# The first two blocks of an input projection become a pair with one group of seven products, and the recurrence behind them starts three steps later

## The chip, the cores and the metric

The kernel runs on one core of one Trainium2 chip. The time is device microseconds of that core for one execution; a stated time is the median of several runs. The engines are PE (TensorE, matrix products into PSUM accumulators), DVE (VectorE), ACT (ScalarE), POOL (GpSimd) and SP (SyncE, which here only issues transfers). Each engine works through its own list of instructions in order and waits at an instruction until what it needs is there.

## The reference

One layer of an encoder on x of 256 rows and 2048 columns, in float32. In short:

```
x += 1/2 * SwiGLU(RMSNorm(x))                       # F = 5632 columns
h = RMSNorm(x);  [u | q | k | v] = h @ w_in         # w_in: 2048 x 4096, u, q, k, v of 1024 each
y_ssm = GLU(S5(u))                                  # a diagonal complex recurrence over the rows
y_sb  = StickBreakingAttention(norm(q), norm(k), v)
x += concat(RMSNorm(y_ssm), RMSNorm(y_sb)) @ w_out
x += 1/2 * SwiGLU(RMSNorm(x))
x += RMSNorm((p @ w_ple_proj) * sigmoid(RMSNorm(x) @ w_ple_gate))
```

The change touches `u = h @ w_in[:, :1024]` and when the recurrence S5(u) begins.

## The kernel before

**Products.** A float32 product is made from three products of a reduced type. Each operand is split into a high part (a rounded copy, a cast on ACT) and a low part (the difference, on DVE): `split`, lines 182 and 185. PE then adds up left-high times weight-high, left-low times weight-high (line 345) and left-high times weight-low (line 340). The left side is the activation, normed only by its gain; the row scale of the RMSNorm (`xn.rs(t)`) is applied when the accumulator is read. The 256 rows are two row tiles (t = 0, 1) of 128.

**Blocks, quarters, halves.** Weight columns are worked in blocks of 512. The 2048 rows of a weight are 16 k tiles, four to a quarter. SP loads a quarter (`raw`, 1 MB, five buffers, of which two hold x through this stage); it is split in halves of two k tiles (`weight_pair`, tiles `whi` and `wlo`, four of each). `gemm_block` runs a block: for each quarter it takes the activation's part, loads and splits the weight, and for each half issues 12 products of 512 columns (two row tiles, two k tiles, three products).

**Seven products.** Elsewhere in this kernel (the two FFNs and the final gate) two blocks are a pair (`Seven`). On one k quarter, with the two k halves, the two row tiles and the two blocks as a 2 x 2 by 2 x 2 product, `chunk` makes seven products in place of eight, in Winograd's form. It needs sums of weights: `t1 = b11 + b12`, `t2 = t1 + b22`, `t4 = t2 + b21` on DVE, and `b12 + b22` by a transfer that adds into SBUF, issued by POOL (line 597). It needs sums of the activation, made by `whole_rows` and `sum_forms` (line 486). Each of the seven has its own split, and is 6 products of 512 columns into one of eight accumulator banks: 1, 2, 4 and 5 are the four `acc` buffers, 6 with 7 and 3 with 8 the two double `aux` buffers. `column` runs quarters of one block of the pair in the plain way. What comes out is then put together: `opened` (bank 1, 6, 7), `gated` (2, 4, 5), and a last sum with banks 3 and 8. In the FFNs `weight_pair` takes three further pairs from a second pool (`ring`, `turns`); `single`, a form of `chunk`, runs with the four alone.

**Steps.** `step()` is called behind each half of a plain block, and four times in a `chunk`. `put_off(n, fn)` runs fn in the (n+1)-th step from then. So everything beside the main products is placed by counting steps: the RMSNorm's parts (`Normed`), the recurrence, the attention. From this program order a planner makes each engine's list, by what it reckons to be ready; instructions under `pin` keep their order.

**Around the change.** After the first FFN `s5_main` sets the recurrence up, then two blocks make u, then four blocks q0, k0, q1, k1, then two blocks v: 16, 32 and 16 steps. Quarter 3 of the normed x comes through PE transposes two steps after the FFN's last block (line 435), the other quarters through DVE transposes and transfers. `u_block` reads a block's two accumulators with the row scale (line 1121). `u_turn` (line 1127) transposes the result in blocks of 32, and `u_part` (line 1138) moves it by eight transfers on SP into `ua[n]`, where the recurrence reads it. The recurrence has four quarters q; each is a chain of stages counted from `a0 = 13 + 8 * q`: `states` (PE, line 1186), `forth` (1203), `scan` (1213), `back`, `outputs` (PE, 1241), `fetch`, `join`, `gelu`. It keeps three tiles `rt` in turn. Its constants come by transfers from scratch memory: `m1`, `rot`, `cp` on SP (line 1151), and `m3` from `scr_h` on POOL (line 1159). Behind the last `gelu`, `channels` sends the result through 32 transfers on SP (line 1287) into `zt`, four a step; `glu_in` reads it 11 steps behind the q and k blocks. `qk_turn` transposes q and k on PE into an `aux` buffer, five steps behind each of their blocks.

## Time and profile before

| what | value |
|---|---|
| median of 3 runs | 1814.45 us (1814.3 to 1815.05) |
| the profiled execution: its time, its span | 1816.04 us, 1814.3 us |
| PE busy | 1806.9 us, 8914 products |
| PE weight loads busy | 1497.1 us |
| DVE busy | 1573.8 us |
| ACT busy | 1065.2 us |
| POOL busy | 104.8 us |
| HBM read and written | 372.41 MB, 10.88 MB |
| first load of `w_in` issued | 681.4 us |
| first product of u | 705.95 us |
| first product of the recurrence | 746.37 us |
| first transfer of `zt` | 847.88 us |

The page of the profile shows one execution. A row of its groups, or of the order of time, names the line of the kernel, the engine, the operation, output and inputs by the program's names, and shapes. In the order of time the first two numbers are start and duration in us, and a bracket at the end gives how long the engine stood idle before it and what ended this. Records of products last 0.39 us and overlap, since PE works on several at once; the distance between starts is the pace. Waits are inferred from semaphores.

### The profile page before, as it was taken

What the parts mean: (1) busy time and instruction counts of PE and PEld (TensorE: products, weight loads), DVE (VectorE), ACT (ScalarE), POOL (GpSimd) and SP (SyncE); (2) the same over time, 40 slices, a digit from 0 to 9 for tenths busy, and PEclk for the clock granted to TensorE, in tenths of its full rate; (3) what the DMA queues carried; (4) which work ended last, traced back from release to release, by engine and by line L of the source; (5) the groups of instructions that cost most, each with busy time, mean ns of one, the idle gap of its engine ahead of it and who ended that gap; (6) DMA issues with size and microseconds to landing.
All of it is one profiled execution on the core that took longest, in us unless ns stands there. A gap on an engine that the chain in (4) does not pass through costs nothing.

```text
span 1814.3 us, 24211 instructions
## 1 busy us (share of the span) xinstructions
PE 1806.9 (100%) x8914; PEld 1497.1 (83%) x8914; DVE 1573.8 (87%) x1840; ACT 1065.2 (59%) x1240; POOL 104.8 (6%) x160
## 2 busy tenths in 40 slices
PE   9999999999999999999999999999999999999998
PEld 7888888888888888888898888888888888888887
DVE  7998889999998896697567899999999999889875
ACT  7445456555565665456695566555565556566664
POOL 0020100000000001010021000000000000000000
PEclk9999999999999999999999999999999999999999
DMA  9599867787776667674646787786767786666663
GB/s 369 201 307 318 255 225 232 240 269 221 257 269 218 197 234 253 189 254 156 219 146 217 232 295 228 265 271 221 234 232 238 242 271 239 227 209 223 200 244 128
DMA packets 107799, 428.41 MB, mean 236 GB/s; under 512 B 24512, under 2 KB 48352, under 8 KB 65280
## 3 DMA queue, kind: packets, MB, share of 16 engines
q1 hardware_dynamic: 96832, 391.15, 61.2%
q0 software_dynamic: 10560, 35.40, 9.0%
q8 instruction: 70, 1.15, 0.3%
q14 instruction: 49, 0.40, 0.1%
q10 hardware_dynamic: 288, 0.31, 0.1%
HBM read 372.41 MB, written 10.88 MB: 211 GB/s over the span
## 4 chain that ended last, share of the span: by engine, by line
PE 96%; DMA 2%; DVE 1%; SPq 1%; ACT 0%; issue 0%; ACTq 0%; DVEq 0%
PE acc L345 32%; PE acc L340 16%; PE aux L345 15%; PE aux L340 7%; PE acc L529 5%; PE acc L532 5%; PE acc L530 5%; PE aux L532 3%; PE aux L530 3%; PE aux L529 3%; DMA raw<-in_ffn_w_up 1%; SPq L233 0%; DMA sg<-in_turned 0%; PE aux L1241 0%; PE acc L1497 0%; PE acc L1492 0%
## 5 line engine op out<-in xcount | busy, mean ns | idle before, releaser
L185 DVE TENSOR_TENSOR wlo<-raw,whi 128x1024 fp32r<-128x1024 f32 x478 | 578.1, 1222 | 126.8 <-ACT whi L182 123.3
L182 ACT CAST whi<-raw 128x1024 fp32r<-128x1024 f32 x478 | 496.3, 1050 | 295.5 <-PE acc L345 182.7
L345 PE MATMUL acc<-whi,nhi 128*128 128x512 f32 x908 | 356.0, 393 | 0.4 <-ACT whi L297 0.3
L345 PE MATMUL acc<-whi,nlo 128*128 128x512 f32 x908 | 353.4, 390 | 0.0
L340 PE MATMUL acc<-wlo,nhi 128*128 128x512 f32 x908 | 252.9, 389 | 0.6 <-DVE wlo L185 0.5
L185 DVE TENSOR_TENSOR slo<-raw,shi 128x1024 fp32r<-128x1024 f32 x186 | 226.0, 1215 | 16.9 <-ACT shi L182 16.7
L182 ACT CAST shi<-raw 128x1024 fp32r<-128x1024 f32 x186 | 195.1, 1049 | 61.4 <-DMA raw<-in_ffn_w_down 22.3
L345 PEld LDWEIGHTS acc<-whi,nhi 128*128 128x128 f32 x908 | 170.5, 188 | 37.7 <-ACT whi L297 0.7
L340 PEld LDWEIGHTS acc<-wlo,nhi 128*128 128x128 f32 x908 | 170.5, 188 | 36.9 <-DVE wlo L185 1.4
L345 PEld LDWEIGHTS acc<-whi,nlo 128*128 128x128 f32 x908 | 170.8, 188 | 34.8
L182 ACT CAST whi<-sum 128x1024 fp32r<-128x1024 f32 x79 | 83.3, 1054 | 160.1 <-DVE sum L536 143.9
L182 ACT CAST shi<-sum 128x1024 fp32r<-128x1024 f32 x59 | 62.2, 1054 | 101.8 <-DVE sum L536 91.5
L536 DVE TENSOR_TENSOR sum<-sum,raw 128x1024 f32<-128x1024 f32 x92 | 112.1, 1219 | 0.9
L185 DVE TENSOR_TENSOR wlo<-sum,whi 128x1024 fp32r<-128x1024 f32 x79 | 96.2, 1220 | 5.3 <-ACT whi L182 4.5
L597 POOL DMA_DIRECT2D raw<-raw x44 | 38.2, 869 | 1032.6 <-DVE sum L536 714.6
L345 PE MATMUL aux<-whi,nhi 128*128 128x512 f32 x220 | 85.7, 390 | 0.0
L345 PE MATMUL aux<-whi,nlo 128*128 128x512 f32 x220 | 85.6, 389 | 0.0
L185 DVE TENSOR_TENSOR slo<-sum,shi 128x1024 fp32r<-128x1024 f32 x59 | 72.0, 1220 | 1.1 <-ACT shi L182 0.5
L340 PE MATMUL aux<-wlo,nhi 128*128 128x512 f32 x220 | 67.8, 389 | 0.0
L536 DVE TENSOR_TENSOR sum<-raw,raw 128x1024 f32<-128x1024 f32 x46 | 56.0, 1217 | 5.6 <-DMA raw<-in_ffn_w_down 4.6
L345 PE MATMUL acc<-whi,hhi 128*128 128x512 f32 x156 | 60.7, 389 | 0.0
L345 PE MATMUL acc<-whi,hlo 128*128 128x512 f32 x156 | 60.7, 389 | 0.0
(393 smaller groups left out, 3401.3 us busy)
## 6 DMA issues: line engine op xcount, KB each, us to landing
raw<-in_ffn_w_up SPq DMA_DIRECT2D x88, 1024.0 KB, 5.7
raw<-in_ffn_w_down SPq DMA_DIRECT2D x88, 1024.0 KB, 4.9
raw<-in_ffn_w_gate SPq DMA_DIRECT2D x86, 1024.0 KB, 7.2
raw<-in_w_in SPq DMA_DIRECT2D x32, 1024.0 KB, 5.3
raw<-raw POOLq DMA_DIRECT2D x46, 512.0 KB, 5.5
raw<-in_w_out SPq DMA_DIRECT2D x16, 1024.0 KB, 5.0
raw<-in_w_ple_gate SPq DMA_DIRECT2D x16, 1024.0 KB, 5.1
hT<-mid SPq DMA_DIRECT2D x160, 64.0 KB, 4.7
```

The lines of the kernel that those rows point to most:

```text
L182: copy = nc.scalar.copy(hi, src)
L185: rest = nc.vector.tensor_tensor(out=lo, in0=src, in1=hi.bitcast(F32), op=ALU.subtract)
L340: nc.tensor.matmul(ps[t], lhsT=lh, rhs=lo[:, j, cols], start=False, stop=stop and j == 1)
L345: nc.tensor.matmul(ps[t], lhsT=(ahi, alo)[i][:, 2 * h + j, t * P : (t + 1) * P], rhs=hi[:, j, cols], start=start and j == 0 and i == 0, st ...
L529: nc.tensor.matmul(ps, lhsT=lh[j], rhs=hi[:, j], start=begin and j == 0, stop=False)
L530: nc.tensor.matmul(ps, lhsT=ll[j], rhs=hi[:, j], start=False, stop=False)
L532: nc.tensor.matmul(ps, lhsT=lh[j], rhs=lo[:, j], start=False, stop=z in final and j == 1)
L536: nc.vector.tensor_tensor(out=t, in0=x, in1=y, op=ALU.add)
L597: nc.gpsimd.dma_start(b12, b22, accum_op=ALU.add)
```

## The change

The two blocks of u are no longer two calls of `gemm_block` and `u_block`, but one `u_pair` on both with kb = 3:

- side 0 in the plain way on quarters 0 and 1, then `made` (the sums of the activation's quarter 3), then quarter 2;
- the seven products on quarter 3 of both blocks, with the four weight pairs alone (`turns` is None, and `chunk` no longer sets the ring in that case);
- `opened` and `gated` put off to the next step: they read banks 1, 6, 7, 2, 4 and 5; side 0 of u is then scaled and goes to `u_turn`;
- side 1 on quarters 0, 1 and 2, a last sum with banks 3 and 8, scaling, `u_turn`.

The sums take the recurrence's three `rt` tiles (`Spare`). The steps stay 16: six, four and six. The loads of `m1`, `rot` and `cp` for the first quarter of the recurrence go from at once to 3, 6 and 9 steps put off, those of `m3` from 4 to 8, and `a0` from 13 to 16, and with it every stage of the recurrence, its later loads and `zt`.

```diff
-            if ring[0] is None:
+            if ring[0] is None and self.turns:
                 ring[:] = [self.turns, 0]
...
+    class Spare:
+        def __init__(self, pool):
+            self.pool = pool
+
+        def tile(self, shape, dtype, tag, name, bufs):
+            return get(self.pool, "rt", bufs=3).rearrange("p (j n) -> p j n", n=NB)
+
+    def u_pair(pool, xn, w, kb, forms):
+        rows = Spare(pool)
+        us = [com("sg"), com("h")]
+        even, odd = ([u[:, t * NB : (t + 1) * NB] for t in range(TT)] for u in us)
+
+        def made():
+            forms[kb] = sum_forms(rows, whole_rows(rows, xn(kb)), "h")
+
+        def opened(s):
+            nc.scalar.copy(even[0], s.bank(1))
+            nc.vector.tensor_tensor(out=odd[0], in0=s.bank(6), in1=even[0], op=ALU.add)
+            nc.vector.tensor_tensor(out=odd[1], in0=s.bank(7), in1=odd[0], op=ALU.add)
+
+        def scaled(side):
+            u = us[side]
+            for t in range(TT):
+                v = u[:, t * NB : (t + 1) * NB]
+                nc.scalar.activation(v, v, AF.Copy, scale=xn.rs(t))
+            put_off(1, u_turn, pool, side, u)
+
+        def gated(s):
+            for t, (ps, other) in enumerate(((s.bank(2), even[0]), (s.bank(4), odd[1]))):
+                nc.vector.tensor_tensor(out=even[t], in0=ps, in1=other, op=ALU.add)
+            scaled(0)
+            v = us[1].rearrange("p (t n) -> p t n", t=TT)
+            nc.vector.tensor_tensor(
+                out=v, in0=s.bank(5).unsqueeze(1).to_broadcast([P, TT, NB]), in1=v, op=ALU.subtract
+            )
+
+        others = tuple(k for k in range(ND) if k != kb)
+        s = Seven(xn, forms.get, ((w, 0), (w, NB)), rows, None)
+        s.column(0, others[:2])
+        made()
+        s.column(0, others[2:])
+        s.chunk(kb, (*shared, 2, 4))
+        put_off(0, opened, s)
+        put_off(0, gated, s)
+        s.column(1, others, True)
+        nc.vector.tensor_tensor(out=us[1], in0=s.banks[3.8], in1=us[1], op=ALU.add)
+        scaled(1)
...
-        load(0, ("m1", "rot", "cp"))
+        for i, name in enumerate(("m1", "rot", "cp")):
+            put_off(3 + 3 * i, load, 0, (name,))
         for z in range(SL):
-            put_off(4 + z, load_m3, z)
+            put_off(8 + z, load_m3, z)
...
-            a0 = 13 + 8 * q
+            a0 = 16 + 8 * q
...
-    for n in range(2):
-        u_block(pool, n, gemm_block(nm, w_in, n * NB, KD), nm)
+    forms = {}
+    u_pair(pool, nm, w_in, 3, forms)
```

## The prediction

> **What bounds the kernel now.** I read the page first (busy time, then the chain of work that ended last), then tables of busy time by stretch around the input projection, then the order of time of each engine there.

> ```profile
> span 1814.3 us, 24211 instructions
> ...
> PE 1806.9 (100%) x8914; PEld 1497.1 (83%) x8914; DVE 1573.8 (87%) x1840; ACT 1065.2 (59%) x1240; POOL 104.8 (6%) x160
> ...
> PE 96%; DMA 2%; DVE 1%; SPq 1%; ACT 0%; issue 0%; ACTq 0%; DVEq 0%
> ```

> TensorE (PE) is idle for 1814.3 - 1806.9 = 7.4 us in all, and 96% of the chain is its own. A busy PE need not be at its peak, so I look at the stage of the change: columns are PE, weight load, DVE, ACT, POOL (busy us, instructions), granted clock, DMA share, GB/s.

> ```profile
> 700.00:750.00 50.00, 50.00 (x282) 41.05 (x282) 27.15 (x38) 24.86 (x33) 6.08 (x12) 1.00 0.79 254
> ...
> 850.00:870.00 20.00, 20.00 (x90) 16.57 (x89) 8.48 (x14) 9.62 (x12) 0.00 (x0) 1.00 0.37 102
> ```

> PE has no idle time from 700 to 750 and its clock is full; DVE works 27.15 of these 50 us. So the time here is the number of PE products times their pace, plus whatever PE is made to wait. Two starts on the chain, one half quarter (12 products) apart, give the pace:

> ```profile
> 720.60 1.81 PE acc L345 x8
> 723.32 1.81 PE acc L345 x8
> ```

> (723.32 - 720.60) / 12 = 0.227 us for one product of 512 columns.

> **The change, part by part.** *Products of the last quarter.* Two blocks, four k tiles, two row tiles and three products each (hi hi, lo hi, hi lo) are 48; seven groups of two k tiles and three products are 42. Six products go: 6 x 0.227 = -1.36 us on the path. No transposes or other PE work come in. [...]

> *The sum forms of the left side.* `made` must wait for quarter 3 of the normed input. Before:

> ```profile
> 705.95 0.39 PE L345 MATMUL acc<-whi,nhi 128*128 128x512 f32 x1
> ...
> 707.96 1.05 ACT L182 CAST whi<-raw 128x1024 fp32r<-128x1024 f32 x1 [3.93 <-PE acc L345]
> ...
> 714.11 1.03 PE L435 MATMUL aux<-ident,x 128*128 128x128 f32 x8
> 714.90 0.48 PE L345 MATMUL acc<-whi,nhi 128*128 128x512 f32 x1
> ...
> 717.07 1.66 DVE L197 SCALAR_TENSOR_TENSOR nlo<-aux,gains,nhi 128x256 fp32r<-128x256 f32 x4 [0.25 <-ACT nhi L195]
> ```

> Quarter 3 is there at 717.07 + 1.66 = 718.7. The forms are one sum of 1024 elements, four small ones, a cast and a difference. The final gate stage builds the same ones, and only then begins the sums of its seven (L536):

> ```profile
> 1705.65 1.23 DVE L469 TENSOR_TENSOR whole<-nhi,nlo 128x1024 f32<-128x1024 f32 x1 [0.71 <-PE aux L340]
> ...
> 1708.04 0.42 DVE L486 TENSOR_TENSOR rows<-whole,rows 128x256 f32<-128x256 f32 x1
> ...
> 1710.21 1.18 DVE L185 TENSOR_TENSOR hlo<-rows,hhi 128x1024 fp32r<-128x1024 f32 x1
> ...
> 1713.17 1.21 DVE L536 TENSOR_TENSOR sum<-raw,raw 128x1024 f32<-128x1024 f32 x1
> ```

> From start to end 1710.21 + 1.18 - 1705.65 = 5.7 us there, with other DVE instructions before the difference. Without them: 1708.04 + 0.42 - 1705.65 = 2.8 for the five sums, 1.05 for the cast, 1.18: 5.0. So the forms are ready between 723.7 and 724.4. PE's need: the row at 714.90 starts half 3 of the first block; halves 4 and 5 follow at 717.62 and 720.34, so the seven begin at 714.90 + 3 x 2.72 = 723.06. Group 1 uses whole rows; group 5 starts at 723.06 + 1.36 = 724.4 and is the first to need the forms. The margin is between 0.7 us and nothing, so no wait if DVE takes the forms first.

> *Splits and sums of the seven.* Three more splits (cast 1.05 on ACT, difference on DVE) and three sums. DVE's pace in a row of such instructions:

> ```profile
> 237.86 4.62 DVE L185 TENSOR_TENSOR wlo<-raw,whi 128x1024 fp32r<-128x1024 f32 x4
> 242.40 0.68 DVE L1084 TENSOR_TENSOR m<-t,t 128x512 f32<-128x512 f32 x1
> ```

> (242.40 - 237.86) / 4 = 1.14 us each. The seven take DVE (7 + 3) x 1.14 = 11.4 us against 42 x 0.227 = 9.5 us on PE: DVE loses 1.9 us, which its lead must cover. The lead is four weight pairs (the change gives this group no extra ring): the cast at 707.96 waits for PE to release the pair of the half that began at 705.95, so splits run four places ahead. Four places before the seven are groups 1, 5, 6 and 4, 5.4 us of PE. Here the 4.0 us of forms on DVE fall into the same stretch. The accumulators are now read by DVE four times over 512 columns and twice over 1024; such reads cost:

> ```profile
> 1744.55 0.68 DVE L1638 TENSOR_TENSOR e<-acc,e 128x512 f32<-128x512 f32 x1
> ...
> 1746.22 1.23 DVE L1632 TENSOR_TENSOR e<-acc,e 128x1024 f32<-128x1024 f32 x1
> ```

> In all DVE gains 6 x 1.14 (splits, sums) + 4.0 (forms) + 4 x 0.68 + 2 x 1.23 = 16.0 us; 27.15 + 16.0 = 43 of 50, so it fits on average and is tight from 717 to 731.

> What the tightness costs is read from two places that run the seven. With four pairs only, in the first FFN (group starts):

> ```profile
> 230.06 0.39 PE L529 MATMUL acc<-whi,nhi 128*128 128x512 f32 x1
> ...
> 231.44 0.50 PE L529 MATMUL acc<-whi,hhi 128*128 128x512 f32 x1
> ...
> 232.95 0.39 PE L529 MATMUL acc<-whi,nhi 128*128 128x512 f32 x1
> ```

> 1.38 and 1.51 instead of 1.36: 0.17 us lost. At the gate stage's seven, the first column half behind them:

> ```profile
> 1728.58 0.41 PE L345 MATMUL acc<-whi,nhi 128*128 128x512 f32 x1
> ...
> 1730.33 0.39 PE L345 MATMUL acc<-whi,nhi 128*128 128x512 f32 x1
> ```

> (1730.33 - 1728.58) - 1.36 = 0.39 us lost. Bounds for this stage: nothing lost, to 6.1 us (second rival). I take +0.4, the gate stage's value, since it too has the forms just ahead. ACT's additions (four casts, one copy) lie in a stage where it is half idle.

> *Transfers.* Loads on SP stay the same in number. The pair needs quarter 3 of both blocks at once:

> ```profile
> 698.71 1.00 SPq L330 DMA_DIRECT2D raw<-in_w_in  x2
> 705.32 0.33 SPq L330 DMA_DIRECT2D raw<-in_w_in  x1
> 705.74 0.38 SPq L1151 DMA_DIRECT2D m<-scr_m  x1
> ...
> raw<-in_w_in SPq DMA_DIRECT2D x32, 1024.0 KB, 5.3
> raw<-raw POOLq DMA_DIRECT2D x46, 512.0 KB, 5.5
> ```

> These three issues now carry quarter 2 and both quarters 3, landed by 705.32 + 5.3 = 710.6, twelve us ahead; the recurrence's three loads leave this moment, which helps them. The one new transfer (a sum within SBUF, on POOL's queue) can start after the first sum and takes 5.5 us; its user is the last group, at 723.06 + 6 x 1.36 = 731.2. Even if that sum runs only at 722 the transfer is down by about 729. The `scr_h` loads stand behind it on POOL and are first read by `outputs`, much later. Zero.

> *The recurrence, three steps later.* The first inputs wait for the pair, whose first side is complete only when the seven end (723.06 + 9.5 = 732.6): then come four reads by DVE (2.7 us), two scalings by ACT, two transposes, eight issues and their landing:

> ```profile
> 728.85 1.26 ACT L1121 ACTIVATE sg<-acc,sm 128x512 f32<-128x512 f32 x2
> ...
> L1127 DVE STREAM_TRANSPOSE ub<-sg x4: 669/693/704, 730.1 to 756.8; 128x512 f32<-128x512 f32 x4
> ...
> DMA to landing us min/median/max: 2.2/2.4/4.9
> ...
> 731.45 5.00 SPq L1138 DMA_DIRECT2D ua<-ub  x8
> ...
> 746.37 0.32 PE L1186 MATMUL aux<-ua,m 64*64 64x64 f32 x2
> ```

> 732.6 + 2.7 + 1.3 + 1.4 + 5.0 + 2.4 = 745.4. `states(0)` moves from 746.37 by three steps less the saving, 8.2 - 1.4, to about 753. Covered by 7 us; if that cover were gone, each microsecond late is one on PE, which runs `states` in its own order. At the far end the 32 `zt` issues move too:

> ```profile
> 847.88 15.18 SPq L1287 DMA_DIRECT2D zt<-mid  x24
> 863.18 0.51 SPq L330 DMA_DIRECT2D raw<-in_w_in  x1
> ...
> 868.70 2.00 ACT L182 CAST whi<-raw 128x1024 fp32r<-128x1024 f32 x2 [6.74 <-DMA raw<-in_w_in]
> ...
> 871.76 0.48 PE L345 MATMUL acc<-whi,nhi 128*128 128x512 f32 x1
> ```

> A weight load of `v` stands behind 24 of them; its cast ends at 869.75 for a half that starts at 871.76, 2.0 us to spare. Later by three steps the block meets another load. Bounds: none, to all 32 ahead of one: 8 more at 15.18 / 24 = 0.63, less 2.0, is 3.0 us. I take zero: the issues go out four a step from step 52 on, and the next block's first load comes before step 57, behind 20 of them and not 24. The recurrence's DVE work ends some 7 us later, in or near 850 to 870, where DVE is free for 11.5 of 20 us. The loads of `m1`, `rot` and `cp` go onto SP at steps 4, 7 and 10 in place of at once: three issues of 0.4 us, whose users are `states` and later.

> **Sum.** -1.36 + 0.4 = -0.96 us: the profiled span 1814.3 becomes 1813.3, and its execution, 1816.04 with what lies around it, 1815.1. That execution is 1.6 us over the runs' median of 1814.45; on the median the sum gives 1813.5.

> **Rivals.** *The saving is eaten.* Small waits at the forms and in the seven together cost 1 to 3 us: 1814.1 to 1816.1. For it: DVE is short by 1.9 us over the seven, with the forms on top. Against: the two places above lost 0.17 and 0.39. *The forms stand behind the seven's own work (slower).* DVE runs what its planned order says. If the three sums and the splits of groups 1, 5 and 6 (6 x 1.14 = 6.8 us) precede the forms, group 5 starts 6.8 - 0.7 = 6.1 us late: 1814.45 - 1.36 + 6.1 = 1819.2. It turns against the change from 1.4 us of wait. Against: at the gate stage the forms came first (L486 and `hlo` before L536). [...] *The `zt` block starves the `v` products*: 1813.5 + 3.0 = 1816.5; against it, the order reckoned above. *The pair relieves the turning of q and k*: `states` and `outputs` no longer hold both wide accumulators when `qk_turn` wants one. PE shows no idle there to recover: 1813.1 at best.

> **How the numbers follow.** Forecast 0.62 and relief 0.04 (1812.8 to 1814.1), saving eaten 0.18, forms late 0.09, `zt` 0.04, something faster than any row explains 0.03. A measurement of this kernel tells about 0.2% (3.6 us) from no change: forecast, relief, eaten saving and most of `zt` lie within it, forms late above it. Hence faster 0.03, same 0.87, slower 0.10. The range goes from 1812.6, which is 1813.1 less half a microsecond of spread between runs, to 1816.4, which holds the eaten saving.

> **What would show it.** PE 8908 instructions; DVE about 1858; POOL 161. Seven group starts 1.36 apart near 723 to 732, with the forms' `hlo` ended before group 5; a longer first step there names the forms, longer later ones the splits. `states(0)` near 753 without a gap before it, `zt` near 855. I am wrong if PE shows a wait above 2 us in the seven, at `states`, or in `v`.

## The result, and the profile after

| | before | after |
|---|---|---|
| median | 1814.77 us (6 runs, 1814.3 to 1816.51) | 1824.69 us (6 runs, 1823.58 to 1825.64) |
| ratio to before, 95% interval | | 1.0054 (1.0043 to 1.0065) |
| span of the profiled execution | 1814.3 us | 1823.7 us |

The change makes the kernel about 10 us slower. The prediction was 1813.5 us, no measurable difference, with a range up to 1816.4: wrong in sign and outside its range.

The first row of the page after: six products fewer, as said, yet PE is busy longer and idle longer.

```profile
PE 1809.1 (99%) x8908; PEld 1496.8 (82%) x8908; DVE 1591.4 (87%) x1858; ACT 1068.2 (59%) x1244; POOL 107.5 (6%) x161
```

The table by stretch of the kernel after (PE, weight load, DVE, ACT, POOL, clock, DMA share, GB/s) shows the two large losses:

```profile
720.00:740.00 20.00, 18.04 (x76) 13.71 (x75) 18.79 (x22) 11.46 (x13) 3.47 (x5) 1.00 0.57 162
770.00:776.00 6.00, 2.08 (x10) 1.42 (x8) 5.91 (x7) 2.82 (x3) 3.38 (x4) 0.99 0.51 206
776.00:784.00 8.00, 7.43 (x56) 5.71 (x58) 5.59 (x6) 2.93 (x4) 0.00 (x0) 0.58 0.66 252
```

In the kernel before, PE is busy for all of the same three stretches, and its clock is 1.00 in each.

PE's order of time after, with the rows that wait:

```profile
722.89 0.39 PE L529 MATMUL acc<-whi,nhi 128*128 128x512 f32 x1
...
724.82 0.49 PE L529 MATMUL acc<-whi,hhi 128*128 128x512 f32 x1 [0.41 <-ACT hhi L182]
725.77 0.50 PE L529 MATMUL aux<-whi,hhi 128*128 128x512 f32 x1 [0.46 <-ACT whi L182]
726.61 0.50 PE L530 MATMUL acc<-whi,hlo 128*128 128x512 f32 x1 [0.33 <-DVE hlo L185]
...
729.95 0.50 PE L529 MATMUL acc<-whi,nhi 128*128 128x512 f32 x1 [0.76 <-ACT whi L182]
...
735.59 0.39 PE L345 MATMUL aux<-whi,nhi 128*128 128x512 f32 x1
...
759.48 0.33 PE L1230 MATMUL aux<-ua,m 64*64 64x64 f32 x2
...
769.19 1.08 PE L340 MATMUL acc<-wlo,nhi 128*128 128x512 f32 x4
...
776.57 2.07 PE L340 MATMUL acc<-wlo,nhi 128*128 128x512 f32 x4 [4.49 <-DVE wlo L185]
778.45 0.63 PE L345 MATMUL acc<-whi,nhi 128*128 128x512 f32 x1
778.87 0.63 PE L345 MATMUL acc<-whi,nlo 128*128 128x512 f32 x1
...
783.29 0.27 PE L1285 MATMUL aux<-ua,m 64*64 64x64 f32 x2
...
901.58 0.50 PE L345 MATMUL acc<-whi,nhi 128*128 128x512 f32 x1 [0.65 <-ACT whi L182]
```

- **The seven** run from 722.89 to 735.59, 12.70 us where 42 x 0.227 is 9.53: **+3.2 us**. The four waits shown add up to 1.96. A bracket counts from the end of the last record, 0.39 - 0.227 = 0.16 us behind the start at which the next product was due, which adds 4 x 0.16; and the first steps behind a wait are longer than 0.227 (from 726.61 to 726.95 it is 0.34, and from 729.95 to 730.29).
- **The last quarter of q's first block.** Its low product follows the one at 769.19 by 2.72, so it is due at 771.91; it starts at 776.57: **+4.7 us**.
- **The clock behind that wait.** The granted clock is 0.58 from 776 to 784; from 778.45 to 778.87 one product takes 0.42 us and not 0.227. The 16 products between 776.57 and 783.29 take 6.72 us where 16 x 0.227 is 3.63: **+3.1 us**.
- **In `v`** one wait of 0.65.

With the six products' -1.36 that is +10.3. In the order of time of DVE the same late instruction, the first of the final gate's forms, stands at 1705.65 before (a row the prediction quotes) and here at

```profile
1715.44 1.22 DVE L469 TENSOR_TENSOR whole<-nhi,nlo 128x1024 f32<-128x1024 f32 x1
```

9.8 us later, so the list is complete to half a microsecond.

What DVE did in the two places, in order of time after:

```profile
716.49 1.66 DVE L197 SCALAR_TENSOR_TENSOR nlo<-aux,gains,nhi 128x256 fp32r<-128x256 f32 x4 [0.72 <-ACT nhi L195]
718.07 1.22 DVE L185 TENSOR_TENSOR wlo<-raw,whi 128x1024 fp32r<-128x1024 f32 x1
719.20 1.22 DVE L469 TENSOR_TENSOR rt<-nhi,nlo 128x1024 f32<-128x1024 f32 x1
...
721.47 1.22 DVE L536 TENSOR_TENSOR rt<-raw,raw 128x1024 f32<-128x1024 f32 x1
...
723.05 1.23 DVE L536 TENSOR_TENSOR rt<-rt,raw 128x1024 f32<-128x1024 f32 x1
724.20 1.22 DVE L185 TENSOR_TENSOR wlo<-rt,whi 128x1024 fp32r<-128x1024 f32 x1
725.33 1.22 DVE L185 TENSOR_TENSOR hlo<-rt,hhi 128x1024 fp32r<-128x1024 f32 x1
...
762.76 1.22 DVE L1247 TENSOR_TENSOR rt<-aux,rot 128x1024 f32<-128x1024 f32 x1 [7.08 <-PE aux L1230]
...
768.69 2.29 DVE L1257 TENSOR_TENSOR_SCAN rt<-dec,rt 128x1024 f32<-128x1024 f32 x1
771.01 1.23 DVE L1265 TENSOR_TENSOR rt<-rt,rot 128x1024 f32<-128x1024 f32 x1
...
775.30 5.76 DVE L185 TENSOR_TENSOR wlo<-raw,whi 128x1024 fp32r<-128x1024 f32 x5
```

First place: quarter 3 is normed at 718.1. The forms' last difference (`hlo`) starts only at 725.33, because group 1's split (718.07), t1, t2 and t1's split go in front of it; on ACT, too, t1's cast (722.77) goes before the forms' cast (723.74). Group 5 wants the forms at 724.3. The longest of the four waits in the seven, at 729.95, is for the cast of t4, whose sum DVE runs behind the forms, at 727.60. Second place: `forth` (L1247) waits 7.08 us for `states(0)`; then forth, two splits, scan and back run in one row, and the split that PE waits for comes behind them, at 775.30. That split's weights had been loaded late too (the load left SP at 763.18, behind transfers that wait), so there were several suspects.

### The profile page after: what moved, and what is told of

It reads as the page before. It is cut to its first block, busy times and chain, and to the rows that moved or that the text cites. A ratio compares the mean times of both kernels' runs of the same rounds, so it can differ in the third digit from the quotient of the medians.

```text
span 1823.7 us, 24224 instructions
## 1 busy us (share of the span) xinstructions
PE 1809.1 (99%) x8908; PEld 1496.8 (82%) x8908; DVE 1591.4 (87%) x1858; ACT 1068.2 (59%) x1244; POOL 107.5 (6%) x161
## 3 DMA queue, kind: packets, MB, share of 16 engines
HBM read 372.41 MB, written 10.88 MB: 210 GB/s over the span
## 4 chain that ended last, share of the span: by engine, by line
PE 55%; SPq 1%; ACT 1%; DVE 0%; issue 0%; DMA 0%; ACTq 0%; DVEq 0%
PE acc L345 17%; PE aux L345 8%; PE acc L340 8%; PE aux L340 4%; PE acc L532 3%; PE acc L530 3%; PE acc L529 3%; PE aux L532 2%; PE aux L530 2%; PE aux L529 2%; SPq L1331 1%; PE acc L1542 0%; PE acc L1537 0%; PE acc L1533 0%; PE aux L1285 0%
## 5 line engine op out<-in xcount | busy, mean ns | idle before, releaser
L185 DVE TENSOR_TENSOR wlo<-raw,whi 128x1024 fp32r<-128x1024 f32 x478 | 578.3, 1225 | 119.3 <-ACT whi L182 113.4
L182 ACT CAST whi<-raw 128x1024 fp32r<-128x1024 f32 x478 | 495.9, 1050 | 306.2 <-PE acc L345 183.6
L345 PE MATMUL acc<-whi,nhi 128*128 128x512 f32 x868 | 341.1, 394 | 2.2 <-ACT whi L287 1.0
L345 PE MATMUL acc<-whi,nlo 128*128 128x512 f32 x868 | 338.4, 391 | 0.0
L340 PE MATMUL acc<-wlo,nhi 128*128 128x512 f32 x868 | 245.0, 391 | 4.5 <-DVE wlo L185 4.5
L185 DVE TENSOR_TENSOR slo<-raw,shi 128x1024 fp32r<-128x1024 f32 x186 | 226.8, 1219 | 16.3 <-ACT shi L182 15.3
L182 ACT CAST shi<-raw 128x1024 fp32r<-128x1024 f32 x186 | 195.1, 1049 | 65.9 <-DMA raw<-in_ffn_w_down 19.7
L340 PEld LDWEIGHTS acc<-wlo,nhi 128*128 128x128 f32 x868 | 163.5, 189 | 39.7 <-DVE wlo L185 5.4
L345 PEld LDWEIGHTS acc<-whi,nhi 128*128 128x128 f32 x868 | 163.3, 188 | 38.8 <-ACT whi L287 1.7
L345 PEld LDWEIGHTS acc<-whi,nlo 128*128 128x128 f32 x868 | 163.5, 188 | 33.3 <-DVE nlo L288 0.2
L182 ACT CAST whi<-sum 128x1024 fp32r<-128x1024 f32 x79 | 83.3, 1054 | 159.1 <-DVE sum L536 140.2
L182 ACT CAST shi<-sum 128x1024 fp32r<-128x1024 f32 x59 | 62.1, 1053 | 100.8 <-DVE sum L536 95.1
L536 DVE TENSOR_TENSOR sum<-sum,raw 128x1024 f32<-128x1024 f32 x92 | 112.5, 1222 | 0.9
L185 DVE TENSOR_TENSOR wlo<-sum,whi 128x1024 fp32r<-128x1024 f32 x79 | 96.5, 1224 | 5.2 <-ACT whi L182 4.5
L345 PE MATMUL aux<-whi,nhi 128*128 128x512 f32 x244 | 95.0, 390 | 0.0
L345 PE MATMUL aux<-whi,nlo 128*128 128x512 f32 x244 | 95.0, 389 | 0.0
L340 PE MATMUL aux<-wlo,nhi 128*128 128x512 f32 x244 | 75.1, 389 | 0.0
L185 DVE TENSOR_TENSOR slo<-sum,shi 128x1024 fp32r<-128x1024 f32 x59 | 72.1, 1222 | 1.1 <-ACT shi L182 0.5
L345 PE MATMUL acc<-whi,hhi 128*128 128x512 f32 x156 | 60.7, 389 | 0.0
L345 PE MATMUL acc<-whi,hlo 128*128 128x512 f32 x156 | 60.7, 389 | 0.0
L345 PE MATMUL aux<-whi,hhi 128*128 128x512 f32 x152 | 59.1, 389 | 0.0
## 6 DMA issues: line engine op xcount, KB each, us to landing
raw<-in_ffn_w_up SPq DMA_DIRECT2D x88, 1024.0 KB, 5.4
raw<-in_ffn_w_down SPq DMA_DIRECT2D x88, 1024.0 KB, 4.9
raw<-in_ffn_w_gate SPq DMA_DIRECT2D x86, 1024.0 KB, 7.2
raw<-in_w_in SPq DMA_DIRECT2D x32, 1024.0 KB, 5.6
raw<-raw POOLq DMA_DIRECT2D x47, 512.0 KB, 5.6
raw<-in_w_out SPq DMA_DIRECT2D x16, 1024.0 KB, 5.0
raw<-in_w_ple_gate SPq DMA_DIRECT2D x16, 1024.0 KB, 5.1
```

What stands on the lines that cost most here:

```text
L182: copy = nc.scalar.copy(hi, src)
L185: rest = nc.vector.tensor_tensor(out=lo, in0=src, in1=hi.bitcast(F32), op=ALU.subtract)
L340: nc.tensor.matmul(ps[t], lhsT=lh, rhs=lo[:, j, cols], start=False, stop=stop and j == 1)
L345: nc.tensor.matmul(ps[t], lhsT=(ahi, alo)[i][:, 2 * h + j, t * P : (t + 1) * P], rhs=hi[:, j, cols], start=start and j == 0 and i == 0, st ...
L536: nc.vector.tensor_tensor(out=t, in0=x, in1=y, op=ALU.add)
```

## The experiments

Theory 1: the load is late, because SP's list is in order and holds transfers that wait. Theory 2: the split is late, because it stands behind scan and back in DVE's list. Theory 3: the seven lose because the forms of quarter 3 come late. Theory 4, formed after the first four runs: `states(0)` has a later place in PE's list. Counted in the lists, it stands 105 products behind the seven in the change, against 84 behind the end of side 0 in the kernel with the seven on quarter 2; in the trace of the change, (759.48 - 735.59) / 0.227 = 105. In the expectations "the third q load" is that of the last quarter of q's first block, which is the fourth. All ratios are to the kernel before, measured again beside each experiment: its median lay between 1813.96 and 1814.77 us. The profiles of the change and of its variants that keep quarter 3 are up to 1.6 us apart already where the seven begin (721.62 to 723.22), so times of two kernels are compared through the ratio, or from the start of the seven.

**The later recurrence alone** (before, with the three edits of the step numbers):

```diff
-        load(0, ("m1", "rot", "cp"))
+        for i, name in enumerate(("m1", "rot", "cp")):
+            put_off(3 + 3 * i, load, 0, (name,))
...
-            put_off(4 + z, load_m3, z)
+            put_off(8 + z, load_m3, z)
...
-            a0 = 13 + 8 * q
+            a0 = 16 + 8 * q
```

> Only the later recurrence (three steps) and its later loads; the two input blocks are computed as before, 8914 products. Theory 1 (the wait near 772 comes from the recurrence's new place: on SP a weight load for q stands behind the `ua` transfers of the second block and the `m1` load): the wait and the slower clock are here too, some 7.7 us, and the `zt` wait of 0.8 in `v`: about 1823. Rival (the wait comes from the pair, whose two sides are turned within a few microseconds of each other): little is lost here, 0 to 1 us: 1814.5 to 1815.5.

1815.11 us, 1.0003 (0.9994 to 1.0012), PE idle 0.10 us between 700 and 910. `states(0)` starts at 752.25, near the 753 of the prediction. The rival holds: the wait is not the price of the three steps. It takes the pair.

**`ua` on POOL's queue** (the change, one line):

```diff
-                nc.sync.dma_start(ua[n][p1 : p1 + HC, :], ub[p0 : p0 + HC, :])
+                nc.gpsimd.dma_start(ua[n][p1 : p1 + HC, :], ub[p0 : p0 + HC, :])
```

> The change, with the `ua` transfers issued by POOL instead of SP. Theory 1 (in-order SP: the third q load waits behind `ua` and `m1`, which wait for others): that load leaves near 755 and not 763, no PE wait above 1 us near 772, clock 1.00: 1824.7 - 7.7 = 1817.0. Theory 2 (DVE: the split of that load stands behind the recurrence's scan in DVE's order, whenever the load lands): the wait near 772 stays within 1 us of its 4.65: 1824 to 1825.

1817.20 us, 1.0015 (1.0005 to 1.0025), no wait near 772, clock 1.00: theory 1's number to 0.2 us. It was a hit for the wrong reason. DVE's list had changed as well (splits stand on both sides of the scan, and one inside back), and `states(0)` started 97 products behind the seven, so this run can't tell theory 1 from the others; the next but one can.

**One step earlier** (`a0 = 15 + 8 * q`):

> The change, with the recurrence one step (2.7 us) earlier, 15 and not 16. Theory 1: the third q load leaves SP about 2.7 us earlier, so that the PE wait falls from 4.65 to about 1.9 us and no longer lowers the clock: 1824.7 - 2.7 - 3.1 = 1818.9. If the lower clock has nothing to do with the length of the wait: 1824.7 - 2.7 = 1822.0. Theory 2 (DVE order sets the wait): no change, 1824 to 1825.

1821.74 us, 1.0040 (1.0025 to 1.0055). `states(0)` kept its 105 products and started at 759.82, the load left at 767.89 behind seven `ua` transfers, and PE waited 3.44 us for the cast. The number is that of "the clock has nothing to do with it", but the clock did fall (0.83 from 770 to 780): none of the three expectations had the mechanism. A step number does not set the place.

**The second `m1` load behind the q load**:

```diff
-                put_off(a0 - 4, load, q, ("m1", "rot"))
+                put_off(a0 - 4, load, q, ("rot",))
+                put_off(a0 + -2, load, q, ("m1",))
```

> The change, with the second `m1` load put off by two steps, so that it stands behind the third q load on SP, and nothing else moved: DVE and PE keep their order there. Theory 1 (the q load is late because it stands behind `m1`, which waits for `states(0)` on PE): the load leaves at 760.6 and not 763.2, the PE wait falls from 4.65 to about 2 us, the clock stays at 1.00: 1824.7 - 2.6 - 3.1 = 1819.0. Theory 4 (PE's planned order has `states(0)` 105 products behind the seven and not 84; forth, scan and back on DVE start from it, and the split of the third q load stands behind them on DVE whenever it lands): the wait stays at 4 to 5 us with the lower clock: 1824 to 1825.

1823.23 us, 1.0050 (1.0034 to 1.0065). The order of time of this kernel:

```profile
759.81 0.53 SPq L330 DMA_DIRECT2D raw<-in_w_in  x1
...
765.01 2.00 ACT L182 CAST whi<-raw 128x1024 fp32r<-128x1024 f32 x2 [8.20 <-DMA raw<-in_w_in]
...
774.38 5.75 DVE L185 TENSOR_TENSOR wlo<-raw,whi 128x1024 fp32r<-128x1024 f32 x5
...
775.65 2.07 PE L340 MATMUL acc<-wlo,nhi 128*128 128x512 f32 x4 [4.51 <-DVE wlo L185]
```

This profile runs 0.9 us ahead of the change's (its seven begin at 721.96). Less that, the load left 2.4 us earlier and the cast ran 2.9 us earlier (768.82 in the change), and yet the split came behind back at the same place and PE still waited 4.51 us. **Theory 1 falls**: the late load was real and cost nothing. The time is 9.1 us above that of the kernel before, where the change's is 9.9; the clock came back sooner here (0.73 from 778 to 780 and 1.00 from 780, where the change has 0.50 up to 782), see the last section.

**`ua` on ACT's queue** (as above, with `nc.scalar.dma_start`):

> The change, with the `ua` transfers issued by ACT instead of SP. In this kernel's planned order `states(0)` stands 84 products behind the seven, as with the seven on quarter 2, while the splits on DVE still stand behind forth, scan and back. Theory 4 (the place of `states(0)` decides): no PE wait above 1 us near 772, clock 1.00, and the loss in the seven stays: 1824.7 - 7.7 = 1817. Theory 2 (the splits' place behind the scan decides by itself): the wait stays, 1823 to 1825. ACT's casts behind eight issues may cost up to 2 us more.

1822.27 us, 1.0042 (1.0028 to 1.0055). `states(0)` stood at 84 and the wait came all the same:

```profile
754.14 1.16 PE L1230 MATMUL aux<-ua,m 64*64 64x64 f32 x64
...
759.10 1.22 DVE L1247 TENSOR_TENSOR rt<-aux,rot 128x1024 f32<-128x1024 f32 x1
...
770.51 4.62 DVE L185 TENSOR_TENSOR wlo<-raw,whi 128x1024 fp32r<-128x1024 f32 x4
...
771.77 2.07 PE L340 MATMUL acc<-wlo,nhi 128*128 128x512 f32 x4 [3.12 <-DVE wlo L185]
```

`states(0)` is done at 755.3, but DVE's list now has more in front of `forth`, which starts at 759.10 without an idle moment. So the place of `states(0)` is not enough by itself. What counts is when the row from forth to the split begins on DVE. The row is 775.30 + 1.14 - 762.76 = 13.7 us in the change, and 770.51 + 1.14 - 759.10 = 12.6 here, with one split fewer in it. From forth to PE's need there are 771.91 - 762.76 = 9.2 us in the change (short by 4.5, waited 4.49) and 768.06 - 759.10 = 9.0 here (short by 3.6; PE's product starts 3.7 late).

**Back behind the two splits** (the change; `rests` holds the splits' differences in the order recorded, and `issue_after` forces an order in the lists):

```diff
+        def held(q):
+            with tc.issue_after(rests[-1]):
+                back(q)
...
+                if q == 0 and stage is back:
+                    steps, stage = 6, held
                 put_off(a0 + steps, stage, q)
```

> The change, with `back` of the recurrence's first quarter (L1265 to L1270) issued only after the two splits of the last quarter of q's first block (the load that earlier expectations called the third is the fourth and last of that block); SP's order and the place of `states(0)` on PE stay those of the change. Theory 2 (the split stands behind `back` on DVE): that split runs near 771.0 and not 775.3, the PE wait falls from 4.65 to below 1 us, the clock stays at 1.00: 1824.7 - 4 - 3.1 = 1817.6; `outputs` may now wait up to 2 us for `back`: up to 1819.5. If DVE's order is not the cause: 1823 to 1825.

1820.96 us, 1.0038 (1.0026 to 1.0049), span 1817.9, clock 1.00 all through:

```profile
770.21 2.75 DVE L185 TENSOR_TENSOR wlo<-raw,whi 128x1024 fp32r<-128x1024 f32 x2
...
771.47 1.19 PE L340 MATMUL acc<-wlo,nhi 128*128 128x512 f32 x4
...
777.44 0.27 PE L1289 MATMUL aux<-rt,cp 64*64 64x64 f32 x2 [1.79 <-DVE rt L1270]
```

SP's list and the 105 products are the change's; DVE's list differs. The split starts at 770.21, the wait is gone, and `outputs`, which reads what back made, waits 1.8 us in its place. **Theory 2 holds**: DVE's order, not the load, sets the wait. The span is 5.8 us below the change's, the median 3.7, 1.5 above the upper end expected; against the kernel before it is 7.0 us slower, where the change is 9.9. Its executions spread from 1818.91 to 1821.95 and the profiled one took 1819.7; what the longer ones wait for is not recorded.

**`states(0)` ahead of the second half of q's first quarter** (the change; `states` keeps its last product in `states_last`, and the next half is issued after it):

```diff
         (ahi, alo), (h, hi, lo) = half
+        if states_last:
+            with tc.issue_after(states_last.pop()):
+                return gemm_half(ps, half, ts, start, stop, cols, in_turn)
```

> The change, with one order forced: PE may begin the second half of q's first quarter only after the last product of `states(0)`, so that `states(0)` stands 84 products behind the seven and not 105. DVE and SP keep the change's order there. Theory 4: forth on DVE starts 21 x 0.227 = 4.8 us earlier against PE's products, the row on DVE from forth to the end of the split (13.7 us) then ends in time, no PE wait above 0.5 us near 772, clock 1.00; the loss in the seven stays: 1824.7 - 4.5 - 3.1 = 1817.1. If the place of `states(0)` is not the cause: 1823 to 1825. If the inputs are not there that early, PE waits at `states(0)` instead: 1818 to 1821.

1816.03 us, 1.0011 (1.0002 to 1.0020):

```profile
753.47 1.16 PE L1235 MATMUL aux<-ua,m 64*64 64x64 f32 x64
...
754.70 1.23 DVE L1254 TENSOR_TENSOR rt<-aux,rot 128x1024 f32<-128x1024 f32 x1 [0.27 <-PE aux L1235]
...
767.25 4.62 DVE L185 TENSOR_TENSOR wlo<-raw,whi 128x1024 fp32r<-128x1024 f32 x4
```

And the stretch that lost most, in its table:

```profile
770.00:776.00 6.00, 6.00 (x115) 5.00 (x114) 4.25 (x4) 4.30 (x6) 0.00 (x0) 1.00 0.90 336
```

With DVE's and SP's lists around it as in the change, 21 products' worth of earlier start (21 x 0.227 = 4.8 us) removes the whole second loss. The time is 1.1 us better than expected, but most of that is the kernel before, which measured 0.65 us less beside this run than beside the change: the 1.9 us that are left against it are the loss in the seven (12.72 us, as in the change) less the six products, 3.2 - 1.36. `states(0)` starts at 753.47 without a wait: its inputs were there. So the second loss came from `states(0)` standing later than it had to, through DVE's row behind it. Why the planner put it there is not shown; the inputs' reckoned arrival is the likely reason.

**The seven on quarter 2**, with the forms made before the direct quarter 3:

```diff
         made()
-        s.column(0, others[2:])
-        s.chunk(kb, (*shared, 2, 4))
+        s.chunk(kb, shared)
         put_off(0, opened, s)
+        s.column(0, others[2:], True)
         put_off(0, gated, s)
...
-    u_pair(pool, nm, w_in, 3, forms)
+    u_pair(pool, nm, w_in, 2, forms)
```

> The change, with the seven on quarter 2 instead of 3, so that the sum forms of the left side are ready some 10 us before their use. Theory 3 (the seven took 12.70 us instead of 9.52 because forms, sums and splits all came late behind quarter 3): the seven take 9.5 to 10 us, and everything behind comes about 2.8 us earlier: 1821.9 if the wait near 772 stays as it is. Rival (DVE is simply short over any seven with four weight pairs, 10 instructions of 1.14 us for 9.5 us of products): 11.4 us or more for the seven, 1823.4 to 1824.7.

1814.02 us, 0.9998 (0.9988 to 1.0007): both losses gone, 8 us better than expected. Its order of time:

```profile
712.73 1.22 DVE L185 TENSOR_TENSOR hlo<-rt,hhi 128x1024 fp32r<-128x1024 f32 x1
...
717.04 0.39 PE L529 MATMUL acc<-whi,nhi 128*128 128x512 f32 x1
...
718.40 0.39 PE L529 MATMUL acc<-whi,hhi 128*128 128x512 f32 x1
...
726.56 0.39 PE L345 MATMUL acc<-whi,nhi 128*128 128x512 f32 x1
...
754.19 1.23 DVE L1247 TENSOR_TENSOR rt<-aux,rot 128x1024 f32<-128x1024 f32 x1 [2.10 <-PE aux L1230]
```

The forms end at 713.9, 4.5 us before group 5 at 718.40, and the seven take 726.56 - 717.04 = 9.52 us. Here too DVE takes t1 between the forms' pieces, and DVE is busy 9.9 of the 10 us from 710: neither that order nor a full DVE costs anything while there is time. Theory 3 holds and its rival falls. The second loss went with it, because here `states(0)` stands at 84, with DVE's and SP's lists around it as in the change.

**The seven on quarter 1** (the same with kb = 1: `made`, one direct quarter, the seven, the two other quarters):

> The change, with the seven on quarter 1. Theory 3 and 4 (it needs the left side's forms early, and side 0 must not end with the seven): as with quarter 2, 1813.0 to 1814.5, no wait in the seven and none near 772. If an earlier quarter crowds DVE against the norm of quarters 2 and 3: waits of 1 to 3 us near 705 to 720 and 1815 to 1817.

1817.41 us, 1.0020 (1.0011 to 1.0029): the second case, 0.4 us above its upper end. There the forms come late in another way (PE waits 1.27 us for `hlo` at 713.77 and 1.21 for a cast at 718.67, 2.54 us idle from 710 to 720); no wait near 772.

**t1 before the norm** (the change; load and t1 move ahead of `made`, and `chunk` takes them):

```diff
+        s.column(0, others[2:])
+        raws = s.load(kb)
+        ready = raws, s.add(raws[0], raws[2])
         made()
-        s.column(0, others[2:])
-        s.chunk(kb, (*shared, 2, 4))
+        s.chunk(kb, (*shared, 2, 4), ready)
```

> The change, with the first sum of the seven (t1, 1.14 us on DVE) computed before the norm of quarter 3 and not between the pieces of the forms. If DVE's work behind quarter 3 (forms, t1, t2 and a split in one row) sets the loss in the seven: the forms' last difference ends about 1.2 us earlier and the seven take 11.3 to 12.0 us and not 12.70; all else as in the change: 1823.3 to 1824.0. If the forms alone set it: no change, 1824.7.

1821.14 us, 1.0039 (1.0024 to 1.0054). t1 ran at 709.44, so the weights were there and DVE had time for it. The only wait left in the seven:

```profile
721.96 0.39 PE L529 MATMUL acc<-whi,nhi 128*128 128x512 f32 x1
...
724.56 0.50 PE L530 MATMUL acc<-whi,hlo 128*128 128x512 f32 x1 [0.81 <-DVE hlo L185]
...
732.85 0.39 PE L345 MATMUL aux<-whi,nhi 128*128 128x512 f32 x1
```

They take 732.85 - 721.96 = 10.89 us, 1.8 less than in the change and more of a gain than expected. So much of the first loss was DVE's own order behind quarter 3. Whether the 1.4 left are the forms alone is not shown: t1's split (719.43) and t2 (722.15) still run between the forms' pieces, and `hlo` starts at 723.29. The wait near 772 stayed (4.13 us).

**Both edits together**, t1 before the norm and `states(0)` ahead:

> The two edits together: the first sum of the seven before the norm of quarter 3, and `states(0)` ahead of the second half of q's first quarter. If the two losses are all and add: 1817.1 - 1.8 = 1815.3 (the six products' 1.36 less, 1.4 left in the seven, 0.5 to 0.8 in `v`). If removing the one moves the other (PE earlier against DVE): waits of 1 to 2 us, 1816 to 1818.

1814.35 us, 1.0003 (0.9993 to 1.0012): the two losses add, and without them the change, with its own quarter and steps, runs in the time of the kernel before as far as this measurement can tell. It is 1 us better than expected, again mostly by the kernel before (1814.12 here). Not everything is gone: the seven take 10.87 us, and PE waits 1.07 us in `v`, so that the six products' saving does not show.

**Two groups of seven**, on quarters 0 and 2 (12 products fewer):

```diff
...
+        made(0)
+        s.chunk(0)
+        s.column(0, (1,))
+        made(2)
+        s.chunk(2, shared)
         put_off(0, opened, s)
+        s.column(0, (3,), True)
         put_off(0, gated, s)
+        s.column(1, (1, 3), True)
...
-            a0 = 16 + 8 * q
+            a0 = 16 + 8 * q + 1 * (q == 0)
```

> Groups of seven on quarters 0 and 2 and none on quarter 3, the first step of the recurrence (and only it) one step later: 8902 products, 12 fewer than before. If DVE has room for 16 us more between 690 and 745: -2.7 us, 1811.8. If DVE is full there (with the seven on quarter 2 alone it is busy 8.5 to 9.9 of each 10 us from 700 to 740): waits of 3 to 6 us in the second group and 1815 to 1818.

1834.28 us, 1.0111 (1.0095 to 1.0126), worse than either case expected. The table by stretch:

```profile
710.00:718.00 8.00, 5.74 (x12) 3.89 (x13) 7.94 (x8) 4.75 (x5) 2.14 (x4) 0.50 0.75 198
718.00:720.00 2.00, 2.00 (x7) 1.58 (x6) 2.00 (x3) 2.00 (x3) 0.59 (x1) 0.60 0.18 49
```

PE waits 5.44 us for the forms of the first group, until 712.01; its clock is 0.50 from 710 to 718 and 0.60 in the two us behind (at half from about 709.4 to 719.6, an estimate from slices of 2 us); and it waits again before 734.17 (1.42 us), 743.92 (2.29) and, in q, 790.03 (4.85). The forms of quarter 0 had no products of u in front of them to hide behind: DVE starts them at 706.45, behind an add of the FFN's last block (L765) that waits 4.12 us for PE, and the seven had begun at 705.05. A saving of 0.227 us a product doesn't pay for one uncovered row on DVE.

No version beat the kernel before by more than its measurement can tell. The seven on quarter 2 beats the change by 10 us and equals the kernel before (0.9998).

## Why the prediction was wrong, step by step

Of the change's time 4.7 + 3.1 = 7.8 us come from the later recurrence, which the sum had at nothing, and 3.2 us from the seven, which it had at 0.4. With the first of these taken away (`states(0)` ahead) the kernel ran in 1816.03 us, inside the range that was given.

- **Six products, -1.36 us: right.** With the seven on quarter 2 the seven take 9.52 us against the 10.88 of four halves. Too little to be seen in a median.
- **The forms "between 723.7 and 724.4, so no wait if DVE takes the forms first": the condition failed.** DVE didn't; t1, t2 and t1's split stood between the pieces. The forms ended at 725.33 + 1.14 = 726.5. This is the rival "the forms stand behind the seven's own work", with four of its six instructions in front (group 1's split too), at 3.2 us and not 6.1. The term **+0.4**, taken from the gate stage, measured **+3.2**. The margin had been reckoned as between 0.7 us and nothing; with a margin that may be nothing, and a condition on DVE's order that was taken over from another stage, the chance of 0.09 was too low.
- **Transfers "zero": the cost right, the reason wrong.** The recurrence's loads did not leave that moment: SP sent `m1`, `rot` and `cp` at 705.5 to 706.8, and a second `rot` with them. But t1 could run at 709.4 with the same order of transfers, so the weights were there in time.
- **"`states(0)` moves by three steps less the saving, to about 753": the step that failed.** It came at 759.48. Of these 6.3 us, 21 products (4.8 us) are its place in PE's list, and the late seven in front of it account for the rest. A stage does not move by its step number alone: the planner makes the list, and why it chose this place is not shown. With the order forced `states(0)` did start at 753.47, with its inputs there, so the reckoning of `ua` held and that of the list did not.
- **"The recurrence's DVE work ends some 7 us later, in or near 850 to 870, where DVE is free": I looked at the far end alone.** At the near end its first row of 13.7 us stands in front of a split that PE waits for. The prediction asked of the wait it feared (at `states`) who is late next, and did not ask it of a row that is merely moved. This is the second loss, 4.7 us and 3.1 us of clock, and no rival had it.
- **The `zt` block: zero taken, 0.65 us of wait found in `v`, by another way.** SP sent 28 `zt` transfers and not 20 ahead of the load that left at 887.00, and PE did not wait for it; the wait at 901.58 is for a later cast, at 900.49, with ACT busy on other work right up to it. The kernel with `states(0)` ahead has PE without idle time from 860 to 910, and so has the one with a step less, while others wait there 0.18 to 1.07 us, so the wait is no fixed price of the block; what sets it was not tested.
- **The clock.** The sum and the rivals' times count every product at the full pace of 0.227 us. The waits in the seven, at most 0.76 us, left the clock at 1.00 (720 to 740). Behind the wait of 4.49 us it did fall, to 0.50 from 776 to 782, and that cost 3.1 us.
- **What would show it.** "A wait above 2 us in the seven, at `states`, or in `v`" named three places, and the largest wait was in none of them.

## What to carry to other kernels

A stage that is moved later brings its whole row on an in-order engine with it: list what stands behind that row at its new place, for each engine, and compare the row's length (here 13.7 us) with the time from its start to the next use of what is queued behind it (9.2 us). Where a planner makes the lists, a step number is a wish; look in the list, and force the one order that matters. A saving in products is best taken where its preparation has time to spare: the seven on quarter 2, whose forms were there 4.5 us before their use, lost nothing, and those on quarter 3, whose forms ended at 726.5 for a use at 724.3, lost 3.2.

## What the runs showed of the hardware

```profile
774.00:776.00 2.00, 0.00 (x0) 0.00 (x0) 2.00 (x3) 0.00 (x0) 0.42 (x3) 0.98 0.02 8
776.00:778.00 2.00, 1.43 (x3) 1.16 (x4) 2.00 (x3) 1.04 (x1) 0.00 (x0) 0.50 0.00 0
...
782.00:784.00 2.00, 2.00 (x45) 1.44 (x45) 0.53 (x1) 1.88 (x3) 0.00 (x0) 0.81 1.04 432
```

and with `m1` behind the q load:

```profile
774.00:776.00 2.00, 0.35 (x1) 0.35 (x2) 2.00 (x3) 0.33 (x1) 0.00 (x0) 0.91 0.00 0
776.00:778.00 2.00, 2.00 (x6) 1.52 (x6) 2.00 (x3) 0.72 (x1) 0.00 (x0) 0.50 0.19 25
778.00:780.00 2.00, 2.00 (x8) 1.64 (x7) 2.00 (x2) 0.00 (x0) 0.00 (x0) 0.73 0.87 344
```

If each slice is part full and part half clock, an estimate from these clocks is that the half clock lasts 0.08 + 6 + 0.76 = 6.84 us in the first (from 775.9 to 782.8) and 0.36 + 2 + 1.08 = 3.44 us in the second, behind waits of 4.49 and 4.51 us. Estimated in the same way, the other kernels gave 3.40 us (`ua` on ACT's queue, wait 3.12), 3.44 (one step earlier, wait 3.44), 6.84 (t1 before the norm, wait 4.13) and, with two groups of seven, 10.2 (wait 5.44) and, from slices of 10 us, 6.8 (wait 4.85). By the same estimate the fall comes 2.6 us into the wait of 4.13, 2.7 into that of 3.12, and 4.5 into that of 4.51, at its very end. In the shorter waits the tables show a clock of 1.00: 2.29 us (two groups of seven, 740 to 750), 1.79 (back behind the two splits, 776 to 784) and 0.76 (the change, 720 to 740). So behind much the same wait the half clock lasted 6.84 us in one kernel and 3.44 in another, at 0.426 us a product ((781.43 - 778.45) / 7 in the change) in place of 0.227. What sets when the clock falls and when it comes back is not shown; no run varied a wait alone.
